# Where the weights of a two-layer trunk lie in on-chip memory: one fixed distance for the weight-loaded products, a sweep of distances for the weight-streamed ones

## The chip, the cores and the metric

The kernel runs on one core of a Trainium2 chip. The metric is the device time of one execution in microseconds (us); the kernel before takes 2715.84 us, the median of three runs between 2714.43 and 2718.64. The profile and the trace come from one further execution of the same program.

## The reference

The reference is a two-layer trunk on 256 tokens of width 2048, all in float32. Layer 0 is differential attention followed by a gated MLP, layer 1 is a gated DeltaNet followed by a gated MLP; each of the four parts has an RMS norm ahead of it and a residual after it. Almost all arithmetic is in the products with weight matrices:

```python
qkv = h @ w_qkv                       # 2048 -> 6144, attention
... @ w_o                             # 2048 -> 2048
u = causal_dwconv(h @ w_up, conv_w) + conv_b      # 2048 -> 2 * 5504, both layers
(jax.nn.silu(gate) * val) @ w_down    # 5504 -> 2048, both layers
proj = h @ w_in                       # 2048 -> 12352, DeltaNet
... @ w_out                           # 4096 -> 2048
```

The rest (softmax, the causal convolutions, the chunked delta rule with its triangular inverses) is small work on 256 tokens.

## The kernel before

Activations are kept transposed, features on the 128 partitions and the 256 tokens along the free dimension. A float32 product is made of three passes in the reduced type fp32r: each operand is split into a high part (its rounding) and a low part (what is left), and high x high, low x high and high x low are added up in PSUM.

Weights come from HBM in chunks of 128 x 1024 words on SyncE's queue. `weights` (L78) lands a chunk in `raw`, ScalarE rounds it to `whi` (L89), VectorE subtracts to get `wlo` (L90). Each of the three tiles has three buffers. The tiles `whi` and `wlo` have 128 words more than a chunk needs, and the argument `d` says how many words into the tile the chunk begins.

Two helpers make the products on TensorE:

- `dense` (L101) loads a 128 x 128 block of weights into the array and streams 256 tokens of activations past it (L116, L117, L118, one line for each pass). It is used for the query and key blocks, `w_o`, both `w_up`, both `w_down`, `w_in`, `w_out` and the gate block: 6448 blocks, three matmuls each.
- `dense_tok` (L126) does the reverse, where the result is wanted with tokens on the partitions: it loads 128 tokens of activations and streams 512 columns of weights (L137, L138, L139). It is used for the value weights `w_v` (4 calls) and for `w_z` (8 calls), 96 matmuls each.

While the array works on one matmul, the block for the next one is loaded: in the trace every matmul has its LDWEIGHTS record on a row of its own (PEld), and the two rows overlap.

What this case is about is where these operands lie. Call distance x the number of 4-byte words, modulo 128, by which the streaming operand begins further on in its partition than the loaded one. The constants `HP`, `AP` and `OP` (40, 48, 112) are the places at which weights would lie level with the tiles of activations `h`, `ac` and `oc`. `dense` puts the chunk at `place - x`, so that activations stream at distance x from the loaded weights:

```python
hi, lo = self.weights(w[:, k0:k0 + nk, :], [(place - x) % P for x in dist])   # L107
hi, lo = self.weights(w[:, k0:k0 + nk, :], (HP, HP))                          # L131, dense_tok: distance 0
```

Within a call neither the pass, the block nor the column changes the distance modulo 128, since they move addresses by multiples of 128 words. Both parts, `whi` and `wlo`, have the same distance in every call here.

Before the change the distances of `dense` are as follows. The default is 51; it holds for the projection `w_o`, the gate block, and the whole second MLP but for its first block, which has 12. The query and key blocks of the eight heads (L396) and the four blocks b of the DeltaNet (L677, and L669 for `w_out`) go through 13, 42, 45, 12, 13, 42, 45, 12 and 13, 42, 45, 12. The first MLP goes through a list:

```python
ups = [(x, x) for y in (0, 24, 37, 32, 17, 7, 48) for z in BEST for x in (y, z)] + [(13, 13)]   # L262, BEST = 13, 42, 45
downs = [(x, x) for x in (13, 0, 13, 42, 0, 42, 45, 51)]                                        # L263
```

so that its 43 calls of w_up alternate between a value of y and one of 13, 42, 45, and its eight calls of w_down have the eight distances of `downs`. `dense_tok` is at distance 0 throughout.

The order of the work on each engine is that of the program text, with one addition: small work of a head (norms, scores, triangular inverses, delta rule, gates) is written as generators, which are put in a list by `spawn` and taken one step further by `tick` after every chunk of a product (L119, L140). So small matmuls in plain float32 or fp32r stand between the matmuls of the large products, in some stages: the first call after each norm (`norm_stat`, L179 and L181), the attention heads, and the DeltaNet. In the calls of w_up and w_down, but for the first of w_up, none stand.

Of the kernel before, what the change touches and what calls it, by code (L numbers as in the profile page):

```python
# [16 lines left out]
P = 128  # L17
T = 256
D = 2048
KD = D // P  # L20
EPS = 1e-6
CK = 4
BEST = 13, 42, 45
HP, AP, OP = 40, 48, 112
LNEXP = "natural_log_exp_and_others"

# [1 line left out]
class Trunk:  # L28
# [69 lines left out]
    def banks(self):  # L98
        return self.dps.tile([P, 2, 2 * T], F32, tag="ps", name="ps")

    def dense(self, w, kt, acts, place, tiles=2, lead=0, dist=(51, 51)):  # L101


        nc = self.nc
        ps = self.banks()
        for k0, nk in self.chunks(kt, CK, lead):
            hi, lo = self.weights(w[:, k0:k0 + nk, :], [(place - x) % P for x in dist])  # L107
            steps = [(k, c) for k in range(nk) for c in range(tiles)]
            if k0 + nk == kt:
                steps = [(k, c) for c in range(tiles) for k in range(nk)]  # L110
            for k, c in steps:
                a = acts(k0 + k)
                first, last = k0 + k == 0, k0 + k == kt - 1
                s = slice(c * P, (c + 1) * P)
                o = ps[:, c, :T]
                nc.tensor.matmul(o, hi[:, k, s], a[:, 0, :], start=first, stop=False)  # L116
                nc.tensor.matmul(o, lo[:, k, s], a[:, 0, :], start=False, stop=False)  # L117
                nc.tensor.matmul(o, hi[:, k, s], a[:, 1, :], start=False, stop=last)  # L118
            self.tick()  # L119
        return ps  # L120
# [2 lines left out]

        self.nc.vector.tensor_tensor(u, ps[:, :, :T], self.rstd.unsqueeze(1).to_broadcast([P, 2, T]), ALU.mult)  # L124

    def dense_tok(self, w, kt, acts):  # L126

        nc = self.nc
        ps = self.banks()
        for k0, nk in self.chunks(kt, CK // 2):  # L130
            hi, lo = self.weights(w[:, k0:k0 + nk, :], (HP, HP))  # L131
            for k in range(nk):
                a = acts(k0 + k)
                first, last = k0 + k == 0, k0 + k == kt - 1
                for c in range(2):
                    ah, al = (a[:, i, c * P:(c + 1) * P] for i in range(2))
                    nc.tensor.matmul(ps[:, c, :], ah, hi[:, k, :], start=first, stop=False)  # L137
                    nc.tensor.matmul(ps[:, c, :], ah, lo[:, k, :], start=False, stop=False)  # L138
                    nc.tensor.matmul(ps[:, c, :], al, hi[:, k, :], start=False, stop=last)  # L139
            self.tick()  # L140
        return ps
# [92 lines left out]
                done(2 * blk + c)  # L234
            self.add_squares()

    def project(self, w, kt, acts, place, done, final=False, dists=[(51, 51)] * 8):

        n = KD // 2
        for b in range(n):  # L240
            ps = self.dense(w[b], kt, acts, place, dist=dists[b])
            if b < n - final:
                self.add_out(b, ps, done)
                continue
            for c in range(2):
                k = 2 * b + c
                self.nc.vector.tensor_tensor(self.x[:, k, :], ps[:, c, :T], self.x[:, k, :], ALU.add)
                done(k)

    def ffn(self, w_up, w_down, nj, cols_ap, done, final=False):  # L250

        nc = self.nc
        self.spawn(self.norm_stat())
        with self.tc.tile_pool(name="fp", bufs=1) as fp:
            cols = fp.tile([P, 8 * nj + 64], F32, tag="fcols", name="fcols")[:, :8 * nj]
            cols = cols.rearrange("p (t h j) -> p t h j", t=4, h=2)
            nc.scalar.dma_start(cols, cols_ap)
            acts = []
            if final:
                ups, downs = [(12, 12)] + [(51, 51)] * (nj - 1), [(51, 51)] * 8  # L260
            else:
                ups = [(x, x) for y in (0, 24, 37, 32, 17, 7, 48) for z in BEST for x in (y, z)] + [(13, 13)]  # L262
                downs = [(x, x) for x in (13, 0, 13, 42, 0, 42, 45, 51)]  # L263
            rows = self.rows(fp.tile([P, nj * 2 * T + 8], F32R, tag="ac", name="ac"), nj, 0)
            for j in range(nj):
                ps = self.dense(w_up[j], KD, self.h_acts, HP, dist=ups[j])
                c = []
                u = fp.tile([P, 2, T], F32, tag="u", name="u", bufs=2)
                self.merge(ps, u)
                for half in range(2):  # L270
                    o = fp.tile([P, T], F32, tag=f"cv{half}", name="cv", bufs=2)
                    c4 = [cols[:, t, half, j:j + 1] for t in range(4)]
                    self.conv(o, u[:, half, :], c4[:3], c4[3])
                    c.append(o)
                nc.scalar.activation(c[1], c[1], AF.Silu)
                a = c[0]
                nc.vector.tensor_tensor(a, c[0], c[1], ALU.mult)
                ac = rows[j]
                self.split(ac, a)
                acts.append(ac)  # L280
            self.project(w_down, nj, lambda k: acts[k], AP, done, final, downs)

    def attention(self, w_qk, w_v, w_o, nh, dist_ap, ident_ap, qg, kg, lvec, sub, start, done, lambda_init):

        nc, mp = self.nc, self.mp
        with self.tc.tile_pool(name="at", bufs=1) as at:
# [106 lines left out]
            aTs = []  # L393
            for h in range(nh):
                acts, lead = (self.h_acts, 0) if h else (start, 1)
                mine = 2 * ((BEST + (12,))[h % 4],)  # L396
                qn, go = normed(self.dense(w_qk[h], KD, acts, HP, lead=lead, dist=mine), qgs)
                self.spawn(go)
                kn, go = normed(self.dense(w_qk[nh + h], KD, self.h_acts, HP, dist=mine), kg)
                aT = at.tile([P, 384], F32, tag=f"aT{h}", name="aT")  # L400
                self.spawn(weigh(h, qn, kn, go, aT))
                aTs.append(aT)
            for h in range(0, nh, 2):
                pv = self.dense_tok(w_v[h // 2], KD, self.h_acts)
                v = at.tile([P, 2, 2 * T], F32, tag="v", name="v", bufs=2)
                for c in range(2):
                    nc.scalar.mul(v[:, c, :], pv[:, c, :], self.rstdc[:, c:c + 1])
                for i in range(2):
                    self.spawn(values(h + i, v[:, :, i * T:(i + 1) * T], aTs[h + i]))
# [7 lines left out]
    def gdn(self, w_gate, w_in, w_z, w_out, nb, hb, gate_ap, const_ap, hot_ap, conv_col, ng, done):  # L417
# [12 lines left out]
        with tc.tile_pool(name="gd", bufs=1) as gd:  # L430
# [20 lines left out]
            def lin(ps):  # L451
                u = gd.tile([P, 2, T], F32, tag="u", name="u", bufs=2)
                self.merge(ps, u)
                return u
# [211 lines left out]

            def out(b, acts):
                for blk in range(KD // 2):
                    ps = self.dense(w_out[b * (KD // 2) + blk], 2 * hb, lambda k: self.await_(acts, k), OP, dist=2 * ((BEST + (12,))[b % 4],))  # L669
                    self.add_out(blk, ps, done if b == nb - 1 else None)  # L670

            pg = self.dense(w_gate, KD, self.h_acts, HP, tiles=1)
# [1 line left out]
            pend = None  # L674
            for b in range(nb):
                heads = range(b * hb, (b + 1) * hb)
                mine = 2 * ((BEST + (12,))[b % 4],)  # L677
                cc = gd.tile([P, 32, 32], F32, tag="s4", name="Cc", bufs=3)
                nc.gpsimd.memset(cc, 0.0)
                lqs, inv, acts, zts, vts = [], [], [], {}, {}  # L680
# [2 lines left out]
                for op, i in plan + [("v", i) for i in range(1, hb)]:  # L683
                    if op == "k":
                        hq = heads[i]
                        c = convs(lin(self.dense(w_in[hq * 2], KD, self.h_acts, HP, dist=mine)), (hq, nq + hq))
                        self.spawn(keys(hq, c, cc, 2 * i, lqs))
                        if i == hb - 1:
                            self.spawn(invert(cc, lqs, inv))
                    elif op == "z":  # L690
                        gr = groups[i]
                        zt = zts[i] = gd.tile([P, 2, gv, P], F32, tag="vz", name="zt", bufs=4)
                        ps = self.dense_tok(w_z[heads[gr[0]] // 2], KD, self.h_acts)
                        for t in range(2):
                            nc.scalar.activation(zt[:, t].rearrange(flat), ps[:, t, :], AF.Silu,
                                                 scale=self.rstdc[:, t:t + 1])
                    else:
                        gi = i // gh
                        gr = groups[gi]
                        if i == gr[0]:  # L700
                            vt = gd.tile([P, 2, gv, P], F32, tag="vz", name="vt", bufs=4)
                            ready = []
                            self.spawn(group(gi, gr, lqs, inv, vt, ready, zts, acts))
                        hq = heads[i]
                        c = convs(lin(self.dense(w_in[hq * 2 + 1], KD, self.h_acts, HP, dist=mine)),
                                  (2 * nq + 2 * hq, 2 * nq + 2 * hq + 1))
                        self.spawn(to_tokens(c, vt, 2 * (i - gr[0]), ready))
                if pend:
# [204 lines left out]
```

## Time and profile before

| | |
|---|---|
| median of three runs | 2715.84 us (2714.43 to 2718.64) |
| the profiled execution: its time | 2715.1 us |
| the profiled execution: span, first to last instruction | 2713.3 us |
| TensorE clock granted over the span | 0.999 |
| VectorE busy | 1852.9 us (68%) |
| ScalarE busy | 1453.5 us (54%) |
| GpSimd busy | 118.0 us (4%) |
| read from HBM | 476.03 MB, 176 GB/s over the span |

The stages, by the first matmul of each: attention's query and key blocks from 5.9 us, its values (`dense_tok`) from 211.0, `w_o` from 311.1, the first MLP's w_up from 402.0 and w_down from 884.8, the gate block from 1128.2, the DeltaNet from 1134.6, the second MLP's w_up from 2006.3 and w_down from 2475.4.

How to read it: PE is TensorE's row of matmuls and PEld its row of weight loads. Matmuls are pipelined, each is begun before the one ahead of it has left the array, and the ends of the records are modelled; so a busy PE says only that there was always a matmul under way. How fast they follow each other is read from starts: the view of one line in a window gives the number of its instructions, the least, median and greatest duration in ns, and the first and the last start in us. L116 occurs once in three matmuls of `dense`, so the time from the first to the last start, divided by three times the number less one, is the time per matmul. The same rows can be read for L117 and L118, and for L137 in `dense_tok`.

### The profile page before, as it was taken

How to read it: one execution, taken by the hardware profiler on the slowest of the kernel's cores; microseconds unless marked ns; L12 is line 12 of the kernel's file. 1: busy time of each engine (PE TensorE's matmuls, PEld its weight loads, DVE VectorE, ACT ScalarE, POOL GpSimd, SP SyncE). 2: the span in 40 equal slices, each digit the busy share in tenths (PEclk: the TensorE clock that was granted, in tenths of full speed). 3: DMA queues.
4: the chain of work that ended last, by engine and by line, in shares of the span. 5: the costliest groups of instructions: out<-in, count | busy, mean ns of one | idle time of the engine just before them, and what ended most of it. 6: DMA issues, size and time to landing. Idle time of an engine off the chain costs nothing.

```text
span 2713.3 us, 53669 instructions
## 1 busy us (share of the span) xinstructions
PE 2699.1 (99%) x22352; PEld 2628.1 (97%) x22352; DVE 1852.9 (68%) x2719; ACT 1453.5 (54%) x1994; POOL 118.0 (4%) x220
## 2 busy tenths in 40 slices
PE   8999999999999999999999999999999999999999
PEld 8998999999999999999989989999999999999999
DVE  7776566666767554589688688679677777776444
ACT  6555555555555444484574574484465555554333
POOL 0000000000000000012021021021000000000000
PEclk9999999999999999999999999999999999999999
DMA  6555565666666666645355455455456666666665
GB/s 208 168 169 177 157 199 184 188 186 188 191 187 194 178 189 186 184 151 176 123 157 163 140 158 169 140 162 173 128 194 194 195 193 191 196 194 197 204 200 167
DMA packets 135396, 481.62 MB, mean 178 GB/s; under 512 B 15344, under 2 KB 18416, under 8 KB 135152
## 3 DMA queue, kind: packets, MB, share of 16 engines
q1 hardware_dynamic: 134000, 475.57, 57.7%
q8 instruction: 175, 2.87, 0.4%
q10 hardware_dynamic: 1152, 2.61, 0.3%
q14 instruction: 69, 0.57, 0.1%
HBM read 476.03 MB, written 2.10 MB: 176 GB/s over the span
## 4 chain that ended last, share of the span: by engine, by line
PE 99%; ACT 0%; DVE 0%; DMA 0%; issue 0%; ACTq 0%; SPq 0%; DVEq 0%
PE ps L117 27%; PE ps L116 27%; PE ps L118 27%; PE ps L137 3%; PE ps L138 3%; PE ps L139 3%; PE mp L615 2%; PE mp L225 1%; PE mp L503 1%; PE mp L558 0%; PE mp L567 0%; PE mp L480 0%; PE mp L585 0%; PE mp L579 0%; PE mp L594 0%; PE mp L502 0%
## 5 line engine op out<-in xcount | busy, mean ns | idle before, releaser
L90 DVE TENSOR_TENSOR wlo<-raw,whi 128x1024 fp32r<-128x1024 f32 (+2 forms) x909 | 1110.0, 1222 | 670.0 <-ACT whi L89 666.6
L89 ACT CAST whi<-raw 128x1024 fp32r<-128x1024 f32 (+2 forms) x909 | 948.4, 1044 | 1055.0 <-PE ps L118 871.1
L116 PE MATMUL ps<-h,whi 128*128 128x256 f32 x4304 | 1201.2, 279 | 7.5 <-ACT h L151 5.9
L117 PE MATMUL ps<-h,wlo 128*128 128x256 f32 x4304 | 1202.1, 279 | 2.7 <-DVE wlo L90 2.7
L118 PE MATMUL ps<-h,whi 128*128 128x256 f32 x4304 | 1200.5, 279 | 0.0
L116 PEld LDWEIGHTS ps<-h,whi 128*128 128x128 f32 x4304 | 810.6, 188 | 10.3 <-ACT h L151 5.9
L117 PEld LDWEIGHTS ps<-h,wlo 128*128 128x128 f32 x4304 | 811.8, 189 | 6.5 <-DVE wlo L90 3.4
L118 PEld LDWEIGHTS ps<-h,whi 128*128 128x128 f32 x4304 | 811.8, 189 | 1.3
L116 PE MATMUL ps<-ac,whi 128*128 128x256 f32 x1632 | 453.7, 278 | 0.0
L117 PE MATMUL ps<-ac,wlo 128*128 128x256 f32 x1632 | 453.6, 278 | 0.0
L118 PE MATMUL ps<-ac,whi 128*128 128x256 f32 x1632 | 453.5, 278 | 0.0
L117 PEld LDWEIGHTS ps<-ac,wlo 128*128 128x128 f32 x1632 | 307.5, 188 | 0.0
L116 PEld LDWEIGHTS ps<-ac,whi 128*128 128x128 f32 x1632 | 307.5, 188 | 0.0
L118 PEld LDWEIGHTS ps<-ac,whi 128*128 128x128 f32 x1632 | 307.4, 188 | 0.0
L137 PE MATMUL ps<-whi,h 128*128 128x512 f32 x384 | 150.7, 393 | 0.0
L138 PE MATMUL ps<-wlo,h 128*128 128x512 f32 x384 | 150.0, 391 | 0.0
L139 PE MATMUL ps<-whi,h 128*128 128x512 f32 x384 | 149.9, 390 | 0.0
L116 PE MATMUL ps<-oc,whi 128*128 128x256 f32 x512 | 144.3, 282 | 0.0
L117 PE MATMUL ps<-oc,wlo 128*128 128x256 f32 x512 | 143.7, 281 | 0.0
L118 PE MATMUL ps<-oc,whi 128*128 128x256 f32 x512 | 143.7, 281 | 0.0
L206 DVE SCALAR_TENSOR_TENSOR cv<-u,fcols,cv 128x255 f32<-128x255 f32 (+1 forms) x344 | 142.9, 478 | 0.0
L124 DVE TENSOR_TENSOR u<-ps,rstd 128x512 f32<-128x512 f32 x118 | 81.4, 690 | 45.8 <-PE ps L118 45.5
(201 smaller groups left out, 2221.8 us busy)
## 6 DMA issues: line engine op xcount, KB each, us to landing
raw<-w_up SPq DMA_DIRECT2D x344, 512.0 KB, 4.3
raw<-w_down SPq DMA_DIRECT2D x160, 512.0 KB, 4.0
raw<-w_in SPq DMA_DIRECT2D x128, 512.0 KB, 4.1
raw<-w_z SPq DMA_DIRECT2D x64, 512.0 KB, 3.8
raw<-w_out SPq DMA_DIRECT2D x64, 512.0 KB, 3.7
raw<-w_qk SPq DMA_DIRECT2D x63, 512.0 KB, 4.2
raw<-w_v SPq DMA_DIRECT2D x32, 512.0 KB, 3.7
raw<-w_o SPq DMA_DIRECT2D x32, 512.0 KB, 4.4
```

What stands on the lines that cost most here:

```text
L89: nc.scalar.copy(hi, raw)
L90: nc.vector.tensor_tensor(lo, raw, hi.bitcast(F32), ALU.subtract)
L116: nc.tensor.matmul(o, hi[:, k, s], a[:, 0, :], start=first, stop=False)
L117: nc.tensor.matmul(o, lo[:, k, s], a[:, 0, :], start=False, stop=False)
L118: nc.tensor.matmul(o, hi[:, k, s], a[:, 1, :], start=False, stop=last)
L124: self.nc.vector.tensor_tensor(u, ps[:, :, :T], self.rstd.unsqueeze(1).to_broadcast([P, 2, T]), ALU.mult)
L137: nc.tensor.matmul(ps[:, c, :], ah, hi[:, k, :], start=first, stop=False)
L138: nc.tensor.matmul(ps[:, c, :], ah, lo[:, k, :], start=False, stop=False)
L139: nc.tensor.matmul(ps[:, c, :], al, hi[:, k, :], start=False, stop=last)
L206: nc.vector.scalar_tensor_tensor(out[:, j:], u[:, :T - j], taps[n - 1 - j], out[:, j:], ALU.mult, ALU.add)
L225: last = self.nc.tensor.matmul(out, self.onesr, p[:, j], start=i + j == 0, stop=i + j == n)
L615: nc.tensor.matmul(p[:, v, :], l(v), r[:, v, :], start=i == 0, stop=i == len(terms) - 1)
```

## The change

All lists and arguments of distances for `dense` go; its default becomes 45 (180 bytes) in place of 51, and nothing overrides it. `dense_tok` gets an argument `dists`, four distances for a call, each for two chunks (24 matmuls) one after the other. They are taken from a list `TOK`, so that the 12 calls together use its first 48 entries once each: 1 to 31 without the multiples of four, 33 to 47, and 49 to 57. No instruction is added or removed, no tile changes its size, and no order of work is written otherwise. The core of the diff:

```diff
-BEST = 13, 42, 45
+TOK = [x for x in range(64) if x % 4 or x > 32 and x not in (32, 48)]
...
-    def dense(self, w, kt, acts, place, tiles=2, lead=0, dist=(51, 51)):
+    def dense(self, w, kt, acts, place, tiles=2, lead=0, dist=(45, 45)):
...
-    def dense_tok(self, w, kt, acts):
+    def dense_tok(self, w, kt, acts, dists):
...
-        for k0, nk in self.chunks(kt, CK // 2):
-            hi, lo = self.weights(w[:, k0:k0 + nk, :], (HP, HP))
+        for i, (k0, nk) in enumerate(self.chunks(kt, CK // 2)):
+            hi, lo = self.weights(w[:, k0:k0 + nk, :], 2 * ((HP + dists[i // 2]) % P,))
...
-            ps = self.dense(w[b], kt, acts, place, dist=dists[b])
+            ps = self.dense(w[b], kt, acts, place)
...
-            if final:
-                ups, downs = [(12, 12)] + [(51, 51)] * (nj - 1), [(51, 51)] * 8
-            else:
-                ups = [(x, x) for y in (0, 24, 37, 32, 17, 7, 48) for z in BEST for x in (y, z)] + [(13, 13)]
-                downs = [(x, x) for x in (13, 0, 13, 42, 0, 42, 45, 51)]
...
-                ps = self.dense(w_up[j], KD, self.h_acts, HP, dist=ups[j])
+                ps = self.dense(w_up[j], KD, self.h_acts, HP)
...
-                mine = 2 * ((BEST + (12,))[h % 4],)
-                qn, go = normed(self.dense(w_qk[h], KD, acts, HP, lead=lead, dist=mine), qgs)
+                qn, go = normed(self.dense(w_qk[h], KD, acts, HP, lead=lead), qgs)
...
-                pv = self.dense_tok(w_v[h // 2], KD, self.h_acts)
+                pv = self.dense_tok(w_v[h // 2], KD, self.h_acts, TOK[2 * h:2 * h + 4])
...
-                        ps = self.dense_tok(w_z[heads[gr[0]] // 2], KD, self.h_acts)
+                        ps = self.dense_tok(w_z[heads[gr[0]] // 2], KD, self.h_acts, TOK[16 + 8 * b + 4 * i:20 + 8 * b + 4 * i])
```

The calls for the keys, `w_in` and `w_out` lose their `dist=` in the same way.

More of the change, by code (lines that the diff above doesn't have):

```diff
@@ L235, in add_out, with project @@
             self.add_squares()
-    def project(self, w, kt, acts, place, done, final=False, dists=[(51, 51)] * 8):
+    def project(self, w, kt, acts, place, done, final=False):
         n = KD // 2
         for b in range(n):
-            ps = self.dense(w[b], kt, acts, place, dist=dists[b])
+            ps = self.dense(w[b], kt, acts, place)
             if b < n - final:
@@ L280, in ffn @@
                 acts.append(ac)
-            self.project(w_down, nj, lambda k: acts[k], AP, done, final, downs)
+            self.project(w_down, nj, lambda k: acts[k], AP, done, final)
     def attention(self, w_qk, w_v, w_o, nh, dist_ap, ident_ap, qg, kg, lvec, sub, start, done, lambda_init):
@@ L395, in attention @@
                 acts, lead = (self.h_acts, 0) if h else (start, 1)
-                mine = 2 * ((BEST + (12,))[h % 4],)
-                qn, go = normed(self.dense(w_qk[h], KD, acts, HP, lead=lead, dist=mine), qgs)
+                qn, go = normed(self.dense(w_qk[h], KD, acts, HP, lead=lead), qgs)
                 self.spawn(go)
-                kn, go = normed(self.dense(w_qk[nh + h], KD, self.h_acts, HP, dist=mine), kg)
+                kn, go = normed(self.dense(w_qk[nh + h], KD, self.h_acts, HP), kg)
                 aT = at.tile([P, 384], F32, tag=f"aT{h}", name="aT")
@@ L668, in out @@
                 for blk in range(KD // 2):
-                    ps = self.dense(w_out[b * (KD // 2) + blk], 2 * hb, lambda k: self.await_(acts, k), OP, dist=2 * ((BEST + (12,))[b % 4],))
+                    ps = self.dense(w_out[b * (KD // 2) + blk], 2 * hb, lambda k: self.await_(acts, k), OP)
                     self.add_out(blk, ps, done if b == nb - 1 else None)
@@ L676, in gdn @@
                 heads = range(b * hb, (b + 1) * hb)
-                mine = 2 * ((BEST + (12,))[b % 4],)
                 cc = gd.tile([P, 32, 32], F32, tag="s4", name="Cc", bufs=3)
@@ L685, in gdn @@
                         hq = heads[i]
-                        c = convs(lin(self.dense(w_in[hq * 2], KD, self.h_acts, HP, dist=mine)), (hq, nq + hq))
+                        c = convs(lin(self.dense(w_in[hq * 2], KD, self.h_acts, HP)), (hq, nq + hq))
                         self.spawn(keys(hq, c, cc, 2 * i, lqs))
@@ L704, in gdn @@
                         hq = heads[i]
-                        c = convs(lin(self.dense(w_in[hq * 2 + 1], KD, self.h_acts, HP, dist=mine)),
+                        c = convs(lin(self.dense(w_in[hq * 2 + 1], KD, self.h_acts, HP)),
                                   (2 * nq + 2 * hq, 2 * nq + 2 * hq + 1))
```

## The prediction

> **What bounds the kernel.** I read the page first, then TensorE's waits, the groups of instructions, and last single lines in windows of a stage.
>
> ```profile
> span 2713.3 us, 53669 instructions
> ...
> PE 2699.1 (99%) x22352; PEld 2628.1 (97%) x22352; DVE 1852.9 (68%) x2719; ACT 1453.5 (54%) x1994; POOL 118.0 (4%) x220
> ...
> PE 99%; ACT 0%; DVE 0%; DMA 0%; issue 0%; ACTq 0%; SPq 0%; DVEq 0%
> ```
>
> ```profile
> PE ps L116 <- ACT h L151: 5.9, 1, 5.9
> PE ps L117 <- DVE wlo L90: 2.7, 3, 1.4
> ```
>
> The chain of waits that ends last is 99% TensorE, and TensorE's longest waits, both in the start, sum to 8.6 us. So nothing feeds it too late; the time is the number of its matmuls times the pace at which they follow. A busy share can't tell that pace. The groups tell the numbers, and the mean duration of one in ns (behind the busy time):
>
> ```profile
> L117 PE MATMUL ps<-h,wlo 128*128 128x256 f32 x4304 | 1202.1, 279 | 2.7 <-DVE wlo L90 2.7
> L116 PE MATMUL ps<-ac,whi 128*128 128x256 f32 x1632 | 453.7, 278 | 0.0
> L116 PE MATMUL ps<-oc,whi 128*128 128x256 f32 x512 | 144.3, 282 | 0.0
> L137 PE MATMUL ps<-whi,h 128*128 128x512 f32 x384 | 150.7, 393 | 0.0
> ```
>
> With three lines each, that is 19,344 matmuls of `dense` and 1,152 of `dense_tok`. One ns on each of the former is 19.3 us, on each of the latter 1.2 us.
>
> The kernel before runs the same call at several distances, so its trace already holds the main answer. L116 in single calls of w_down, 86 in each (so 255 steps of matmuls between its first and last start), by least/median/greatest duration and first and last start; the distances are, in this order, 0, 13, 42, 42, 45, and 51 (a call of the second MLP):
>
> ```profile
> L116 PE MATMUL ps<-ac,whi x86: 280/283/283, 916.6 to 947.2; 128*128 128x256 f32 x86
> L116 PE MATMUL ps<-ac,whi x86: 278/286/287, 947.5 to 979.0; 128*128 128x256 f32 x86
> L116 PE MATMUL ps<-ac,whi x86: 276/276/281, 979.3 to 1008.2; 128*128 128x256 f32 x86
> L116 PE MATMUL ps<-ac,whi x86: 278/279/280, 1039.5 to 1069.3; 128*128 128x256 f32 x86
> L116 PE MATMUL ps<-ac,whi x86: 276/276/285, 1069.6 to 1098.6; 128*128 128x256 f32 x86
> L116 PE MATMUL ps<-ac,whi x86: 276/276/276, 2504.6 to 2533.5; 128*128 128x256 f32 x86
> ```
>
> At distance 0 a matmul takes 30.6 us / 255 = 120.0 ns, at 13 31.5 / 255 = 123.5, at 42 113.3 in one call and 116.9 in another, at 45 113.7 (which includes the passage from the call before: its greatest duration is 285, its median 276), at 51 113.3. The recorded durations go with it: 276 stands for 113.3, 279 for 116.7, 283 for 120.0, 286 for 123.3; the pace is the duration less 163. No wait, engine or transfer differs between these calls; only the place of the weights does. So distance matters, 45 and 51 are at the best pace seen, 113.3, and 13 and 0 are not.
>
> [...]
>
> Distance alone does not fix the pace. Two calls of w_up at distance 13, 32 of L116 in each:
>
> ```profile
> L116 PE MATMUL ps<-h,whi x32: 280/282/283, 752.3 to 763.4; 128*128 128x256 f32 x32
> L116 PE MATMUL ps<-h,whi x32: 276/276/276, 819.5 to 830.0; 128*128 128x256 f32 x32
> ```
>
> The first goes at 11.1 us / 93 = 119.4 ns, the second at 112.9. The sequence of starts falls into a rhythm and keeps it until something disturbs it; which rhythm depends on what came before.
>
> **The change part by part.** Instructions, transfers and order stay; only paces change. All work on the other engines is covered: the second MLP runs at 113.3 already with VectorE, ScalarE and the queues doing the same for each chunk as elsewhere, and w_up there has no wait. So every ns off TensorE's pace counts in full.
>
> *First MLP, to be compared with the second, which has the same calls at 51 (its first block at 12).* L116 over all of w_up and all of w_down, first MLP, then second:
>
> ```profile
> L116 PE MATMUL ps<-h,whi x1376: 276/278/291, 402.0 to 884.4; 128*128 128x256 f32 x197
> L116 PE MATMUL ps<-ac,whi x688: 276/281/287, 884.8 to 1127.8; 128*128 128x256 f32 x172
> L116 PE MATMUL ps<-h,whi x1376: 276/276/363, 2006.3 to 2475.0; 128*128 128x256 f32 x197
> L116 PE MATMUL ps<-ac,whi x688: 276/276/282, 2475.4 to 2709.0; 128*128 128x256 f32 x172
> ```
>
> w_up takes 884.8 - 402.0 = 482.8 us in the first and 2475.4 - 2006.3 = 469.1 in the second: 13.7 less. w_down takes 243.0 and 233.6: 9.4 less. Each MLP's first block at 45 in place of 12 (279 to 276 is 3.3 ns, for 96 matmuls) is 0.3 more, twice 0.3. Sum 23.7 us.
>
> *Attention's heads.* L118 of a head at 45, at 13, at 42 and at 12, with the same small work in each:
>
> ```profile
> L118 PE MATMUL ps<-h,whi x64: 276/276/364, 61.7 to 85.8; 128*128 128x256 f32 x64
> L118 PE MATMUL ps<-h,whi x64: 278/283/365, 111.2 to 136.4; 128*128 128x256 f32 x64
> L118 PE MATMUL ps<-h,whi x64: 276/276/370, 136.8 to 161.1; 128*128 128x256 f32 x64
> L118 PE MATMUL ps<-h,whi x64: 276/278/365, 185.9 to 210.6; 128*128 128x256 f32 x64
> ```
>
> They take 24.1, 25.2, 24.3 and 24.7 us. Two heads have each distance; one of those at 13 is the first, whose query block waits for data, so I count half of it: 1.1 + 0.5 + 2 x 0.2 + 2 x 0.6 = 3.1 us.
>
> *DeltaNet.* Small products break up the calls, so I compare mean durations. L117 of the `w_in` calls of block 0 (distance 13), 2 (45) and 3 (12), then of `w_out` of blocks 0, 2 and 3:
>
> ```profile
> L117 PE MATMUL ps<-h,wlo 128*128 128x256 f32 x257 | 73.6, 286 | 0.9 <-DVE wlo L90 0.9
> L117 PE MATMUL ps<-h,wlo 128*128 128x256 f32 x256 | 71.5, 279 | 0.0
> L117 PE MATMUL ps<-h,wlo 128*128 128x256 f32 x256 | 72.2, 282 | 0.0
> L117 PE MATMUL ps<-oc,wlo 128*128 128x256 f32 x128 | 36.2, 283 | 0.0
> L117 PE MATMUL ps<-oc,wlo 128*128 128x256 f32 x128 | 35.9, 280 | 0.0
> L117 PE MATMUL ps<-oc,wlo 128*128 128x256 f32 x129 | 35.8, 278 | 0.0
> ```
>
> Block 0: 7 ns x 768 + 3 x 384 = 6.5 us. Block 3: 3 x 768 = 2.3, and its `w_out`, which no small work breaks up, 278 less 276 for 384, 0.8: together 3.1. Block 1 at 42 can be at 113.3 or 116.9; at half of that difference for 1152 matmuls, 2 us at most, I take 1.0. Sum 10.6 us.
>
> *`w_o`, gate block, second MLP.* 51 becomes 45, both at 113.3: nothing. The cover of that nothing is that 45 holds its rhythm; if it doesn't, see the third rival.
>
> *`dense_tok`.* The trace has it at distance 0 alone. An unbroken call:
>
> ```profile
> L137 PE MATMUL ps<-whi,h x32: 389/389/389, 1229.9 to 1251.0; 128*128 128x512 f32 x32
> ```
>
> 21.1 us / 93 = 226.9 ns for 512 columns, twice 113.3 for 256. I take that as the pace of the stream itself, free of conflict, because the best pace of `dense` is the same by column; then another distance can only cost. The bounds come from `dense`, the nearest rows: at best distance 0 is as bad here as there, 120.0 against 113.3, and all 48 are good: -6.7 ns x 1152 = -7.7 us. At worst all 48 are as 13 is: +10.2 x 1152 = +11.8 us. A mixture of distances, the first w_up's, stood 13.7 us / 4128 = 3.3 ns above the best: +3.8 us if 0 is free, -3.9 if it is not. I hold the first for about three times as likely and take +2.0.
>
> *Slow rhythm at 45.* After a small product at 45 the pace can catch in 120:
>
> ```profile
> L116 PE MATMUL ps<-h,whi x16: 282/283/283, 1532.9 to 1538.3; 128*128 128x256 f32 x16
> ```
>
> Counting the starts, one such catch in about 40 unbroken runs at 45 (the first at 61.7 us, the last at 1950.6), over after 71 matmuls at the next small product. With some 150 runs in the new kernel, I add three more of 30 matmuls at 6.7 ns: +0.6.
>
> Sum: -23.7 - 3.1 - 10.6 + 2.0 + 0.6 = -34.8 us. The profiled execution's 2715.1 us (span 2713.3) becomes 2680.3; the median of the runs, 2715.84, is 0.7 above it and becomes 2681.0.
>
> **The rivals.**
>
> *`dense_tok` gains* (0.15). For it: 13 and 45 changed places with 0 in `dense`, so 0 need not be good here. Against: 226.9 is so near 2 x 113.3. Then -3.9 to -7.7 in place of +2.0: 2671 to 2675. [...]
>
> *`dense_tok` costs more* (0.12): most of the 48 distances fall into slow rhythms, as 13 does in two of the three calls shown. Then +7 to +11.8 in place of +2.0: 2686 to 2691. Against: `dense`'s mixture in w_up stood at a third of that.
>
> *A slow rhythm holds for a stage, and the kernel is slower.* The last small products ahead of a long stretch are those of the norm in the first call of w_up; behind them stand 4128 matmuls of w_up with nothing to break a rhythm, then 2064 of w_down. If 45 catches there at 120, w_up loses 4128 x 6.67 ns = 27.5 us: 2709, still faster (0.04); if the passage to w_down doesn't free it, 6192 x 6.67 = 41.3: 2722 (0.04). It decides against the change from 34.8 / 0.00667 = 5,200 matmuls on. For it: the row at 1532.9, and the same in `w_o` at 51, 24 matmuls long, here by its durations:
>
> ```profile
> L116 PE MATMUL ps<-ac,whi x8: 284/284/364, 319.1 to 321.7; 128*128 128x256 f32 x8
> ```
>
> Against: 45 came to 113.3 in each of its eight undisturbed calls of the first MLP, from many other distances.
>
> [...]
>
> **The numbers.** The forecast as worked out, 2676 to 2685, has 0.63. What a measurement can tell from no change is 0.2%, 5.4 us. Faster: 0.63 + 0.15 + 0.12 + 0.04 = 0.94; same 0.02; slower 0.04. The range 2673 to 2690 takes the forecast, part of the first and most of the second rival; what lies outside is under 0.2.
>
> **What would show it.** Right: both w_up at 469 us and both w_down at 234, L116 to L118 with a median of 276 in every stage, the DeltaNet's L117 at 279 in all blocks. `dense_tok` is read from L137 to L139 by call: medians of 389 to 395, none below 389. Wrong: a stretch of w_up or w_down with 283, or L137 with medians under 389.

## The result and the profile after

The kernel after takes 2685.15 us, the median of four runs (2684.43 to 2685.53); the kernel before took 2715.14 beside it (2713.99 to 2718.64). The ratio is 0.9889, with a 95% interval from 0.9877 to 0.9900: 1.1% faster, by 30.0 us. The forecast was 2681.0 and -34.8 us. The profiled execution took 2684.43 us, with a span of 2682.6, 30.7 under that of before.

The page after, first its span and engines, then three of its groups:

```profile
span 2682.6 us, 53669 instructions
...
PE 2667.8 (99%) x22352; PEld 2591.4 (97%) x22352; DVE 1850.4 (69%) x2719; ACT 1454.5 (54%) x1994; POOL 121.6 (5%) x220
...
L117 PE MATMUL ps<-h,wlo 128*128 128x256 f32 x4304 | 1194.2, 278 | 2.7 <-DVE wlo L90 2.7
...
L116 PE MATMUL ps<-ac,whi 128*128 128x256 f32 x1632 | 450.4, 276 | 0.0
...
L137 PE MATMUL ps<-whi,h 128*128 128x512 f32 x384 | 152.7, 398 | 0.0
```

The counts are those of before. The loaded products fell from 279 to 278 and from 278 to 276 ns, the streamed ones rose from 393 to 398. L116 over the four stages of the MLPs, first w_up, first w_down, second w_up, second w_down:

```profile
L116 PE MATMUL ps<-h,whi x1376: 276/276/281, 402.2 to 870.7; 128*128 128x256 f32 x197
L116 PE MATMUL ps<-ac,whi x688: 276/276/282, 871.0 to 1104.6; 128*128 128x256 f32 x172
L116 PE MATMUL ps<-h,whi x1376: 276/276/363, 1975.9 to 2444.4; 128*128 128x256 f32 x197
L116 PE MATMUL ps<-ac,whi x688: 276/276/282, 2444.7 to 2678.3; 128*128 128x256 f32 x172
```

Both w_up now take 468.8 us (871.0 - 402.2, 2444.7 - 1975.9) and both w_down 233.6. A head that was at 13 takes 24.1 us in place of 25.2, by L118:

```profile
L118 PE MATMUL ps<-h,whi x64: 276/276/364, 111.6 to 135.7; 128*128 128x256 f32 x64
```

In the DeltaNet, L117 in `w_in` of blocks 0 and 3, then in `w_out` of blocks 0 and 3 (before: 286, 282, 283, 278):

```profile
L117 PE MATMUL ps<-h,wlo 128*128 128x256 f32 x256 | 71.7, 280 | 0.9 <-DVE wlo L90 0.9
L117 PE MATMUL ps<-h,wlo 128*128 128x256 f32 x256 | 71.5, 279 | 0.0
L117 PE MATMUL ps<-oc,wlo 128*128 128x256 f32 x128 | 35.6, 278 | 0.0
L117 PE MATMUL ps<-oc,wlo 128*128 128x256 f32 x128 | 35.3, 276 | 0.0
```

And L137 in 24 matmuls of `dense_tok` each, at distances 15, 27, 29, 45 and 49 (before: 389 at distance 0):

```profile
L137 PE MATMUL ps<-whi,h x8: 387/389/390, 280.1 to 284.8; 128*128 128x512 f32 x8
L137 PE MATMUL ps<-whi,h x8: 387/388/391, 1205.5 to 1210.3; 128*128 128x512 f32 x8
L137 PE MATMUL ps<-whi,h x8: 397/398/398, 1211.0 to 1215.9; 128*128 128x512 f32 x8
L137 PE MATMUL ps<-whi,h x8: 394/399/403, 1592.0 to 1597.0; 128*128 128x512 f32 x8
L137 PE MATMUL ps<-whi,h x8: 397/403/403, 1608.8 to 1613.8; 128*128 128x512 f32 x8
```

The pace is again near the duration less 163: 226 at 15, 235 to 240 at 29, 45 and 49, though by the starts 388 stands for 227 as well as 389 does. By the starts of all 48 groups, leaving out the steps that a small product breaks up, the mean paces lie between 227.3 (27) and 239.6 ns (49), and they go by the remainder of the distance by four: 229.5 ns in the mean where it is 3, 233.3 where it is 2, 233.7 where it is 0, 236.4 where it is 1.

Stage by stage, from the first matmul of each to that of the next, in the two profiled executions:

| stage | forecast, us | measured, us |
|---|---|---|
| first w_up, second w_up (first block) | -14.3 | -14.4 |
| first w_down | -9.4 | -9.4 |
| heads 1 to 7 | -2.6 | -2.65 |
| head 0 | -0.5 | +1.55 |
| DeltaNet without `dense_tok` | -10.6 | -11.6 |
| `dense_tok` (290.0 to 296.3) | +2.0 | +6.35 |
| slow rhythm at 45 | +0.6 | in the DeltaNet's |

What is left, -0.6 us, is spread over `w_o`, the gate block and the start.

About 3.2 of the 11.6 us in the DeltaNet are no effect of the change. In the profiled execution before, the granted clock is 0.50 in two stretches of this stage, by the view of windows (from and to, length, TensorE busy with the number of its matmuls, granted clock, share and GB/s of the transfers):

```profile
1143.30:1146.70 3.40, 3.40 (x18) 0.50 0.72 231
1300.30:1303.70 3.40, 3.40 (x18) 0.50 0.06 25
```

In them matmuls of 256 columns follow each other at 213 ns, and one such stretch costs about 1.6 us (see e4). The kernel after has none in this stage. In the stages of the MLPs neither execution has one.

### The profile page after: what moved, and what is told of

Its sections match the earlier page's. It is cut to its first block, busy times and chain, and to the rows that moved or that the text cites. A ratio compares the mean times of both kernels' runs of the same rounds, so it can differ in the third digit from the quotient of the medians.

```text
span 2682.6 us, 53669 instructions
## 1 busy us (share of the span) xinstructions
PE 2667.8 (99%) x22352; PEld 2591.4 (97%) x22352; DVE 1850.4 (69%) x2719; ACT 1454.5 (54%) x1994; POOL 121.6 (5%) x220
## 3 DMA queue, kind: packets, MB, share of 16 engines
q10 hardware_dynamic: 1152, 2.61, 0.3%
## 4 chain that ended last, share of the span: by engine, by line
PE 99%; ACT 0%; DVE 0%; DMA 0%; issue 0%; SPq 0%; DVEq 0%
PE ps L117 27%; PE ps L116 27%; PE ps L118 27%; PE ps L137 3%; PE ps L138 3%; PE ps L139 3%; PE mp L609 2%; PE mp L225 1%; PE mp L497 1%; PE mp L552 0%; PE mp L561 0%; PE mp L474 0%; PE mp L579 0%; PE mp L573 0%; PE mp L588 0%; PE mp L496 0%
## 5 line engine op out<-in xcount | busy, mean ns | idle before, releaser
L116 PE MATMUL ps<-h,whi 128*128 128x256 f32 x4304 | 1193.7, 278 | 8.1 <-ACT h L151 5.5
L117 PE MATMUL ps<-h,wlo 128*128 128x256 f32 x4304 | 1194.2, 278 | 2.7 <-DVE wlo L90 2.7
L118 PE MATMUL ps<-h,whi 128*128 128x256 f32 x4304 | 1193.0, 277 | 0.0
L116 PEld LDWEIGHTS ps<-h,whi 128*128 128x128 f32 x4304 | 808.8, 188 | 10.9 <-ACT h L151 5.5
L117 PEld LDWEIGHTS ps<-h,wlo 128*128 128x128 f32 x4304 | 809.4, 188 | 6.5 <-DVE wlo L90 3.4
L118 PEld LDWEIGHTS ps<-h,whi 128*128 128x128 f32 x4304 | 809.3, 188 | 1.3
L116 PE MATMUL ps<-ac,whi 128*128 128x256 f32 x1632 | 450.4, 276 | 0.0
L117 PE MATMUL ps<-ac,wlo 128*128 128x256 f32 x1632 | 450.3, 276 | 0.0
L118 PE MATMUL ps<-ac,whi 128*128 128x256 f32 x1632 | 450.2, 276 | 0.0
L116 PEld LDWEIGHTS ps<-ac,whi 128*128 128x128 f32 x1632 | 306.3, 188 | 0.0
L117 PEld LDWEIGHTS ps<-ac,wlo 128*128 128x128 f32 x1632 | 306.3, 188 | 0.0
L118 PEld LDWEIGHTS ps<-ac,whi 128*128 128x128 f32 x1632 | 306.2, 188 | 0.0
L137 PE MATMUL ps<-whi,h 128*128 128x512 f32 x384 | 152.7, 398 | 0.0
L139 PE MATMUL ps<-whi,h 128*128 128x512 f32 x384 | 151.9, 396 | 0.0
L116 PE MATMUL ps<-oc,whi 128*128 128x256 f32 x512 | 143.2, 280 | 0.0
L118 PE MATMUL ps<-oc,whi 128*128 128x256 f32 x512 | 142.7, 279 | 0.0
L117 PE MATMUL ps<-oc,wlo 128*128 128x256 f32 x512 | 142.7, 279 | 0.0
```

## The experiments

Theory at the start: the pace of a matmul is set by the distance of its operands, the two parts of the change add up, and 0 was a good distance for the streamed products. The rivals: the time that the forecast missed lies elsewhere; or the streamed products pay for the passing from one distance to the next. The kernels of the first four were each timed against the kernel before; those after them ran once. Single stretches at half clock came in the start and in the DeltaNet, up to four in an execution, so differences of 1.6 us in those stages are read with the clock beside them.

**e1, the loaded products alone**

```diff
-TOK = [x for x in range(64) if x % 4 or x > 32 and x not in (32, 48)]
+TOK = [0] * 48
```

> The kernel after with the streamed products (dense_tok) put back to distance 0; dense at 45 everywhere. Theory (pace is set by distance, the two parts of the change add up, and 0 is a good distance for the streamed products): the 12 calls of dense_tok go back from a mean near 232.7 ns to 226.7, that is 6.4 us, so 2678.8 us. Rival (the time that the forecast missed lies in the small work of the DeltaNet and in the start, not in the streamed products): 2685.

It took 2678.08 us (ratio to before 0.9860, 0.9844 to 0.9877). `dense_tok` takes 290.0 us, as before the change. This is the quickest version of the study, 7 us under the kernel after. Its four times go with the granted clock: 2676.14 and 2676.47 us at 1.000, 2679.69 at 0.999, 2681.39 at 0.998.

**e2, the streamed products alone**: the kernel before, with `TOK` and `dists` as in the change.

> The kernel before with the sweep of 48 distances in dense_tok alone. Theory (parts add up): 2715.1 + 6.4 = 2721.5 us, and the same 24 matmuls have the same pace at each distance as in the kernel after. Rival (the sweep costs only because dense at 45 before it leaves another rhythm): under 2718.

It took 2719.02 us (1.0011, 1.0002 to 1.0021). `dense_tok` takes 296.3 us, +6.36, as in the kernel after; so far the theory. But the whole is 2.5 us under what was expected, and in the trace the difference lies in loaded products, whose distances this kernel leaves alone: the `w_in` calls of block 0 are 4.1 us quicker. The stretch at half clock at 1143.3 in the kernel before is about 1.6 of that, the pace is the rest, 2.5. (`w_out` of blocks 0 and 1 is 1.5 and 1.6 us slower; there e2 has the half clock, at 1483.2 and 1688.0.) The calls after the streamed ones in block 0, at distance 13, in the kernel before (two calls, L116):

```profile
L116 PE MATMUL ps<-h,whi x64: 279/286/287, 1251.7 to 1275.0; 128*128 128x256 f32 x64
```

and the first of them in e2 (where the line is L117), still at 13:

```profile
L117 PE MATMUL ps<-h,whi x32: 276/276/282, 1254.4 to 1265.0; 128*128 128x256 f32 x32
```

286 is 123.3 ns and 276 is 113.3. The matmuls at 13 fell into another rhythm; all that was changed ahead of them is the distance of streamed products. So the parts add up stage by stage, not in the sum.

**e3 and e4, one distance for all streamed products**

```diff
-TOK = [x for x in range(64) if x % 4 or x > 32 and x not in (32, 48)]
+TOK = [45] * 48        # e3; [27] * 48 in e4
```

> The kernel after with all of dense_tok at the one distance 45, the best of dense. Theory (the distance itself costs, and what is good for loaded weights is not so for streamed ones): 237.3 ns as in the 24 matmuls at 45 of the kernel after, 10.6 ns x 1152 = 12.2 us over e1, 2691 us. Rival (it is the passing from one distance to another, four times a call, that costs): with one distance for all it settles near 226.7, 2679 us.

> The kernel after with all of dense_tok at distance 27, where the 24 matmuls of the kernel after came to 227.5 ns between neighbours at 233 to 237. Theory (pace by distance): 0.8 ns x 1152 = 0.9 us over e1, 2679.7 us. Rival (the 24 matmuls at 27 were quick because of the rhythm left by those at 26, not of the distance): the mean of the sweep, 2685 us.

e3 took 2689.89 us (0.9905, 0.9890 to 0.9920), e4 2682.34 (0.9876, 0.9862 to 0.9891). An unbroken call of `dense_tok` in e1, e3 and e4:

```profile
L137 PE MATMUL ps<-whi,h x32: 388/389/390, 1204.8 to 1225.9; 128*128 128x512 f32 x32
```

```profile
L137 PE MATMUL ps<-whi,h x32: 393/400/405, 1208.4 to 1230.5; 128*128 128x512 f32 x32
```

```profile
L137 PE MATMUL ps<-whi,h x32: 387/388/392, 1204.9 to 1226.0; 128*128 128x512 f32 x32
```

At 45 it is 22.1 us / 93 = 237.6 ns with no passing at all, at 27 it is 226.9. All of `dense_tok` takes 301.5 and 290.4 us against 290.0. Here the distance costs, not the passing; and 45, at 113.3 ns for loaded weights, is one of the worst for streamed ones. e4's time is 2.6 us over its expectation, though its streamed products cost 0.5: `w_out` of blocks 1 and 2 is 1.6 us longer in each than in e1, at an unchanged distance 45. That is neither distance nor rhythm: in each of the two e4 has a stretch at half clock, and e1 has none there.

```profile
1655.60:1659.00 3.40, 3.40 (x19) 0.50 0.02 5
1870.70:1874.00 3.30, 3.30 (x17) 0.50 0.00 0
```

The stretches at half clock are four in the profiled execution of e4 (time 2683.33 us, mean clock 0.997) and two in that of e1 (2679.69, 0.999). Why they come is not shown.

**e5, 48 other distances for the streamed products**: `TOK` is the multiples of four up to 32, 48, 58 to 64, 31 more from 65 to 127, and 0.

> As the kernel after, but dense_tok goes through 48 other distances: the multiples of four that it left out, 58 to 64, and a choice from 65 to 127. Theory (the pace is a function of the distance with a period of 64 words, and 226.7 ns is the floor for 512 columns): 64 is as 0, near 226.7, and 65, 67, 71, 75, 79, 83, 91 are as 1, 3, 7, 11, 15, 19, 27 within 1 ns; none below 226. Rival (period 128, or a distance free of conflict that is quicker than 0): 64 differs from 0 by over 2 ns, or some distance goes below 225, in the extreme near 220 as a bound 6.7 ns under the floor.

2686.36 us (before: 2716.67). L137 at distances 64 and 60:

```profile
L137 PE MATMUL ps<-whi,h x8: 389/389/395, 304.5 to 309.3; 128*128 128x512 f32 x8
L137 PE MATMUL ps<-whi,h x8: 388/388/388, 278.8 to 283.5; 128*128 128x512 f32 x8
```

64 comes to 226.7 as 0 does; 67, 71, 75, 79 and 83 have the paces of 3, 7, 11, 15 and 19 within 0.7 ns, and 91 that of 27 within 1.3. 65 lies 1.9 ns under 1, in calls that small products break up. Within this run 124, 125 and 127 have the paces of 60, 61 and 63 within 0.1 ns. So over the distances tried the paces of the streamed products repeat after 64 words, 256 bytes. 60 and 124 reach 226.7 too, and no distance of this run goes under it.

**e6, a sweep for the loaded products**: `dist=2 * (j + 21 * final,)` in the call of w_up, `dense_tok` at 0.

> dense_tok at 0; dense at 45 but for the two w_up: the first goes through 0 to 42, the second through 21 to 63, one distance a call. Theory (113.3 ns is a floor that the distance can only lengthen): no call under 113.3 in the mean, many at 116.7 to 123.3; the two w_up together some 15 to 35 us longer than at 45, about 2700 us. Rival (a better distance than 45 exists): some call has a mean under 113. Distances 21 to 42 come twice, after different neighbours: where the two differ, the rhythm left by the call before decides, not the distance alone.

2719.60 us; the two w_up are 41.9 us longer than in e1, somewhat more than expected. By L116:

```profile
L116 PE MATMUL ps<-h,whi x1376: 276/281/291, 399.7 to 889.6; 128*128 128x256 f32 x197
L116 PE MATMUL ps<-h,whi x1376: 274/281/362, 1990.7 to 2479.5; 128*128 128x256 f32 x197
```

No call is under 113.3 ns in the mean. Of the distances 1 to 63, 13, 42, 45 and 51 reach 113.3, all others lie between 115.7 and 122.2 (0 stands in the first call alone, which small products break up). Of those that come twice, 28, 29 and 32 differ by 1.3 to 3.2 ns between the two w_up, by the rhythm; the others agree within 0.1, but for 21 in the first call of the second w_up. 48, which held 113.3 before the change in three calls, comes out at 117.8 here, behind 47. The floor stands, and it is narrow.

**e7 and e8, 51 or 48 for all loaded products**, with `dist=(51, 51)` or `(48, 48)` as default and `dense_tok` at 0.

> dense at 51 everywhere, dense_tok at 0. Theory (45 and 51 are equal but for how they come out of small products): the two MLPs at 113.3, 2678 us as e1 within 3. Rival of the prediction (a slow rhythm caught behind the norm's products holds for a stage): a w_up at 120, which is 27.5 us more, 2706 us, or with its w_down 2719.

> dense at 48 everywhere, dense_tok at 0. Theory: 48 has the same floor as 45; where small products break up the calls it may come back quicker, so the DeltaNet's first block loses the 1.5 us that it spends at 120 at 45: 2676 to 2678 us. Rival (48 falls into a slow rhythm behind small products): L117 in the DeltaNet over 280 ns, or a w_up at 120 and 2700 us or more.

At 51 it took 2691.37 us, 13 over the expectation. Both w_up hold 113.3; what is lost lies where small products break up the calls, in the heads 1 to 7 (+4.4 us against e1) and the DeltaNet (+7.6). At 48 it took 2717.79, no better than before. L116 of its first w_up and of its first w_down:

```profile
L116 PE MATMUL ps<-h,whi x1376: 276/276/281, 405.6 to 874.0; 128*128 128x256 f32 x197
L116 PE MATMUL ps<-ac,whi x688: 281/281/281, 874.4 to 1117.1; 128*128 128x256 f32 x172
```

All of w_up is at 113.3, all of w_down at 117.8 ns: 2064 matmuls, 9.15 us, and the second MLP's w_down the same again. The DeltaNet, where a gain was hoped for, is 15.8 us longer than in e1, of which three more stretches at half clock are about 5. As for w_down, either a slow rhythm was caught at the passage and held, or 48 is a bad distance with these activations.

**e11, the first call of `w_o` and of each w_down at 45, the rest at 48**

```diff
-            ps = self.dense(w[b], kt, acts, place)
+            ps = self.dense(w[b], kt, acts, place, dist=2 * (48 if b else 45,))
```

> As e8 (dense at 48, dense_tok at 0), but the first of the eight calls of w_o and of each w_down is at 45. In e8 w_up held 113.3 at 48 and all of w_down and of w_o stayed at 117.8. Theory (a rhythm that is caught at the passage and then held; the distance allows both): the call at 45 comes to 113.3 and the seven at 48 behind it keep it, so w_down is 9.1 us quicker in each MLP and w_o some 2.5: near 2697 us. Rival (with these activations 48 is simply a distance of 117.8): the seven calls at 48 stay at 117.8, 2715.

2712.10 us (before: 2714.50). L116 of the first w_up and w_down:

```profile
L116 PE MATMUL ps<-h,whi x1376: 280/281/281, 404.0 to 890.7; 128*128 128x256 f32 x197
L116 PE MATMUL ps<-ac,whi x688: 276/276/282, 891.0 to 1124.7; 128*128 128x256 f32 x172
```

w_down is back at 113.3, in the seven calls at 48 as well: the theory holds. What was not expected is w_up: its own code and distance are those of e8, `w_o` ahead of it now has the quick rhythm, and it caught the slow one and held it for all 4128 matmuls, 487.1 us against 468.8. So a rhythm can last for a whole stage, and can cost 18.3 us there.

**e12, the streamed products at 60**: `TOK = [60] * 48`.

> As e1, but all of dense_tok at distance 60, the one other distance at which 24 matmuls in a row went at 226.7 ns. Theory (226.7 is the floor and 60 reaches it as 0 does): dense_tok within 0.6 us of e1's 290.0, 2678 to 2682 us, what is over coming from the rhythms of the DeltaNet. Rival (0 is the only quick distance, 60 was quick by the rhythm that 59 left): over 293 us for dense_tok.

2683.55 us; `dense_tok` takes 296.0. The rival was right. One call, and a part of an earlier one:

```profile
L137 PE MATMUL ps<-whi,h x32: 394/394/394, 1202.7 to 1224.3; 128*128 128x512 f32 x32
L137 PE MATMUL ps<-whi,h x18: 388/388/398, 246.0 to 258.6; 128*128 128x512 f32 x18
```

Distance 60 has two rhythms, 226.7 and 233.3 ns, and at 60 alone it is mostly in the slow one. Distance 0 came back to 226.7 in every stretch of the kernel before that was long enough to settle.

**e9 and e13, both operands moved together**, by 4 words in e9, by 8 in e13, the distances as in e1:

```diff
-HP, AP, OP = 40, 48, 112
+HP, AP, OP = 44, 48, 112        # e13: 48, 48, 112
...
-        self.place(0)
+        self.place(4)              # e13: place(8)
```

> As e1 (dense at 45, dense_tok at 0), but the activations h lie 4 words further on and the weights that go with them too. Theory (only the distance between the two operands counts): every stage as in e1, w_up at 113.3 and dense_tok at 226.7 ns, 2678 us. Rival (the place of an operand in its own memory line counts): w_up or dense_tok off by more than 2 ns, as the sweep shows for a step of one to four words in the distance, 2690 us or more.

> As e9, but both operands 8 words further on in place of 4 (dense at 45, dense_tok at 0). In e9, at the same distances, w_up went at 116.7 and 120 and dense_tok at 230, while w_down and w_o, whose operands it left alone, stayed at 113.3. Theory, formed from e9 (besides the distance the place of the operands within 8 words counts; w_down's activations lie 8 words off those of w_up, and its 113.3 at 45 shows that a step of 8 does no harm): every stage as in e1, 2678 us. Rival (any move of these activations costs, since their old place happened to be a good one): w_up over 115 ns and dense_tok over 229, 2690 us or more.

e9 took 2741.96 us, over the kernel before (2714.50). So the theory falls here: distance is not all. L116 of its two w_up and of its first w_down, whose operands were not moved:

```profile
L116 PE MATMUL ps<-h,whi x1376: 277/281/284, 410.7 to 892.9; 128*128 128x256 f32 x197
L116 PE MATMUL ps<-h,whi x1376: 277/280/365, 2006.2 to 2501.9; 128*128 128x256 f32 x197
L116 PE MATMUL ps<-ac,whi x688: 276/276/277, 893.2 to 1126.8; 128*128 128x256 f32 x172
```

The first w_up goes at (892.9 - 410.7) / 4125 = 116.9 ns, the second at 120.2; median durations between 276 and 283 hide a pattern of two or three steps here, so the starts are what to read. `dense_tok` takes 293.8 us. e13 took 2678.82 (before: 2716.18), with both w_up at 468.7 and `dense_tok` at 289.8, as e1:

```profile
L116 PE MATMUL ps<-h,whi x1376: 276/276/281, 399.3 to 867.7; 128*128 128x256 f32 x197
L116 PE MATMUL ps<-h,whi x1376: 276/276/364, 1970.4 to 2438.8; 128*128 128x256 f32 x197
```

So at one distance the place of the operands counted as well: the one step of 4 words that was tried changed the pace, the one of 8 did not. The step of 4 words, 16 bytes, cost 13.7 and 27.3 us in the two w_up, and the one of 8, 32 bytes, nothing. The "memory line" of the rival for e9 was the author's guess at a cause; no run shows one.

## Why the prediction was right, point by point

The forecast was 4.1 us too good: 4.35 us of that are `dense_tok`, 2.05 are head 0, and the DeltaNet made up for part of it.

*The pace of TensorE is the time, and distance sets the pace.* Right for the MLPs. The loaded products gave back what the comparison with the second MLP said, to 0.1 us in w_up and w_down, and e1 has all of that gain without the sweep. That distance does nothing, the 0.02 for "same", is ruled out by e3 and e6: e3 differs from e1 in the distance of the streamed products alone, and its `dense_tok` takes 11.5 us more; e6 in that of the two w_up, and they take 41.9 us more. But distance does not set the pace alone. e8 and e11 differ by 18.3 us in one w_up whose instructions and distance are the same, and e9 by 41 us from e1 in its two w_up, at the same distance in another place.

*45 in place of 51 costs nothing.* Right for the MLPs and `w_o`. e7 shows more: 51 everywhere took 11.7 us more than its like at 45, e1, by the profiled executions (two stretches at half clock in each), in the stages where small products break up the calls.

*The DeltaNet.* 10.6 us forecast, 11.6 measured, and that they are so near is luck. Without the two stretches at half clock the gain is about 8.4. The forecast compared mean durations, and its 286 ns for `w_in` of block 0 holds five matmuls of the first of these stretches:

```profile
L117 PE MATMUL ps<-h,wlo x5: 415/415/420, 1143.4 to 1146.0; 128*128 128x256 f32 x5
```

Without them the mean is 283.6, which gives 4.6 ns in place of 7 and 3.5 us in place of 5.4. Block 1, put down for a gain of 1.0, gave 1.5, but the other stretch, in its `w_in`, is 1.6. The slow rhythm at 45 came as feared, but in one piece: the second half of the first `w_in` call of block 0, the second call and most of the third. L116 in the second call, in the kernel after and in e1:

```profile
L116 PE MATMUL ps<-h,whi x32: 282/283/283, 1124.8 to 1136.0; 128*128 128x256 f32 x32
```

```profile
L116 PE MATMUL ps<-h,whi x32: 276/276/277, 1125.7 to 1136.2; 128*128 128x256 f32 x32
```

The same call with the same distance is at 120.0 in one and 113.3 in the other; e3, e4, e5 and e12, also at 45, have it at 113.3 too. About 220 matmuls at 6.7 ns are 1.5 us, more than the 0.6 put down for it.

*Head 0 and the start.* The 1.55 us that it lost are no effect of the distance: head 0 takes 30.7 us in the profile before, but 32.2 in e2, where its distance is that of before, 33.3 in e1 and 30.8 in e5 and e6, which differ from each other only behind it. So it varies by 2.6 us from run to run, and the profiled execution before was among the quick ones. Part of that is the clock: e1, e3, e4, e7, e9 and e11 have a stretch at half clock near 20 us and a head 0 of 32.9 to 33.3 us. The kernel after has none there; what made its head 0 longer is open.

*`dense_tok`, the term that was mis-sized.* The step read "a mixture of distances, the first w_up's, stood 3.3 ns above the best: +3.8 us if 0 is free, -3.9 if it is not", and took +2.0. It measured +6.4. The first half was right: 226.7 ns is the floor, 0 is on it, none of 95 other distances in e5 and the kernel after is under it. The size failed because the mixture was no fair sample: half of its calls were at 13, 42 and 45, picked distances, and those are good for loaded weights only; 45 and 13 cost the streamed ones 10.9 and about 6.7 ns. A fairer sample of `dense` is e6, taken afterwards, where the mean is 41.9 us / 8256 = 5.1 ns over the floor; 1152 times that is 5.9 us, near what the streamed products cost.

*The signs.* Both w_up came at 469 us, both w_down at 234, and L116 to L118 have a median of 276 in the large stages. Two signs were off. L117 in `w_in` is at 279 ns in blocks 2 and 3, but at 280 in block 0 and 282 in block 1. The medians of L137 to L139 by call lie between 391 and 398, none under 389 but some over the 395 that was named.

*The rivals.* That `dense_tok` gains: no run shows it, and 226.7 ns was the least. That it costs more was nearer: 6.4 lies just under that rival's 7. The slow rhythm for a whole stage did not come at 45, but e11 and e9 show that it is real, for 18.3 us at 48 and 27.3 us in e9's second w_up (at 45, its operands moved), the very size that the rival named. That a slow rhythm can be caught at the passage to w_down is shown by e8. In e11 and e9 w_down came free of the slow pace of w_up, but its first call had another distance in the one and its operands another place in the other; that the passage alone frees a rhythm is not shown. Why 45 came back from small products more surely than 51 or 48 is not settled. Nor is it shown why a distance costs: with it moves the place at which the weights are written as well as that at which they are read, and no run parts the two.

## What to carry to other kernels

Where TensorE is the bound and nothing waits, compare the pace of the same matmul in different places of the trace, by starts; here differences of 3 to 10 ns with no wait in them and the same granted clock came from where the operands lay or from a rhythm that was caught there, and moving the weights by a few words cost no instruction (53669 before and after). Choose the place for each kind of product by itself: 45 was among the best for loaded weights (113.3 ns) and one of the worst for streamed ones (237.6, e3). And prefer a place that comes back to the quick rhythm after a disturbance over one that has merely been seen in it: 51 in all loaded products took 11.7 us more than 45 (e7, e1). Before mean durations are compared, look up the granted clock of the stretch: in the DeltaNet five slow matmuls in 256 made up about a third of the difference. Before one kernel's sweep is taken as a forecast for another product, ask how its distances were picked.

## What the runs showed of the hardware

In fp32r the least mean pace was 113.3 ns for 256 columns (e6) and 226.7 for 512 (e5), at a granted clock of 1.00. The pace went with the distance of the two operands, from 113.3 to 123.3 (the kernel before) and from 226.7 to 239.6 ns (49, the kernel after); for the streamed products it repeated after 256 bytes (e5, within 1.9 ns), for the loaded ones a period was not measured. It went with their common place as well: one step of 16 bytes took w_up from 113.3 to 116.9 and 120.2 ns (e9), one of 32 left it at 113.3 (e13). For the streamed products 0 and 60 reached 226.7 (60 not always, 233.3 in e12); in the kernel after, distances of 3 modulo 4 words were quickest in the mean (229.5) and those of 1 slowest (236.4). A sequence of equal matmuls fell into one of two or three rhythms at the same distance (13: 113.3, 120.0, 123.3; 48: 113.3, 117.8; 60, streamed: 226.7, 233.3), and held one for the 4128 matmuls of w_up in e8 (113.3) and e11 (117.8). In the first 13.5 us of the kernel before and 15.4 of the kernel after, matmuls of 256 columns followed at 213 ns. After that the granted clock fell to 0.50 for 3.4 us at a time, none to four times in an execution, in these runs, while matmuls ran, always within the first head or the DeltaNet; matmuls of 256 columns then followed at 213 ns again.
